# RMSNorm and GELU on one core: 48 KB row groups in four buffers, squares shared between ScalarE and VectorE, 1/rms mostly on VectorE, GELU in the group's own turn

## Chip, cores, metric

One core of a Trainium2 chip. The metric is device time in microseconds (us). A single-core program's runs are compared as they are: the granted clock was 1.00.

Short names: ACT is ScalarE, DVE is VectorE, POOL is GpSimd, SP is SyncE (it issues the loads).

## The reference

```python
# x: (8, 1024, 2048) float32, gamma: (2048,), eps = 1e-5
rms = np.sqrt(np.mean(x ** 2, axis=-1, keepdims=True) + eps)
out = gamma * x / rms
return 0.5 * out * (1 + np.tanh(np.sqrt(2 / np.pi) * (out + 0.044715 * out ** 3)))
```

8192 rows of 8 KB: 67.11 MB are read, 67.11 MB written.

## The kernel before

Each of the 128 partitions holds four rows of a group (32 KB); 16 groups go through six buffers. ACT squares and sums each row, POOL makes 1/rms from the four sums, DVE multiplies the rows by gamma in place, and ACT applies GELU with 1/rms as its scale, one group behind the squares.

```python
def scale(g):                      # DVE, in place, gamma broadcast in PSUM
    for r, n in scale_pieces.get(g, [(0, R)]):
        rows = slot[g % SLOTS][:, r : r + n, :]
        nc.vector.tensor_tensor(out=rows, in0=rows, in1=gamma_ps..., op=ALU.mult)
# ... squares (ACT, accum_out=ssq), inverse_rms (six small operations on POOL) cut
for g in range(G + 1):
    if g < G:
        squares(g)
        inverse_rms(g)
        scale(g)
    if g:
        gelu_store(g - 1)                  # one group behind
        if g - 1 + SLOTS < G:
            load(g - 1 + SLOTS)            # when the store has left the buffer
```

Of the kernel before, what the change touches and what calls it, by code (L numbers as in the profile page):

```python
# [1 line left out]

# [4 lines left out]

FP32 = mybir.dt.float32
ALU = mybir.AluOpType
ACT = mybir.ActivationFunctionType  # L10

P = 128
ROWS = 4
SLOTS = 6

GW = 32
CHUNK = 512

NARROW = 128


@with_exitstack
def kernel(
    ctx: ExitStack,
    tc: tile.TileContext,
    x: bass.AP,
    gamma: bass.AP,
    eps: bass.AP,
    out: bass.AP,
):  # L30




    nc = tc.nc
    D = x.shape[-1]
    R = ROWS
    eps_f = float(eps)
    x3 = x.rearrange("b s d -> (b s) d").rearrange("(g p r) d -> g p r d", p=P, r=R)
    o3 = out.rearrange("b s d -> (b s) d").rearrange("(g p r) d -> g p r d", p=P, r=R)  # L40
    G = x3.shape[0]

    sbuf = ctx.enter_context(tc.tile_pool(name="sbuf", bufs=1))
    psum = ctx.enter_context(
        tc.tile_pool(name="psum", bufs=1, space=bass.MemoryType.PSUM)
    )
    slot = [sbuf.tile([P, R, D], FP32, name=f"slot{i}") for i in range(SLOTS)]
    gamma_row = sbuf.tile([1, D // GW, GW + 4], FP32, name="gamma_row")
    ones = sbuf.tile([1, P], FP32, name="ones")
    warm = sbuf.tile([1, 1], FP32, name="warm")  # L50
    power = sbuf.tile([P, R], FP32, name="power")
    ssq = sbuf.tile([P, G, R], FP32, name="ssq")
    rstd = sbuf.tile([P, G, R], FP32, name="rstd")
    ms = sbuf.tile([P, R], FP32, name="ms")
    y = sbuf.tile([P, R], FP32, name="y")
    z = sbuf.tile([P, R], FP32, name="z")
    gamma_ps = psum.tile([P, D], FP32, name="gamma_ps")
    junk = psum.tile([P, D], FP32, name="junk")


    whole = [(R, [(0, R * D)])]
    store_pieces = {
        0: [(R, [(0, NARROW), (NARROW, R * D)])],
        G - 1: [(1, [(r * D, r * D + D)]) for r in range(R)],
    }
    scale_pieces = {G - 1: [(0, 1), (1, 1), (2, 1), (3, 1)]}

    def load(g):
        nc.sync.dma_start(out=slot[g % SLOTS], in_=x3[g])  # L69

    def squares(g):
        for r in range(R):
            nc.scalar.activation(  # L73
                out=junk,
                in_=slot[g % SLOTS][:, r, :],
                func=ACT.Square,
                accum_out=ssq[:, g, r : r + 1],
            )

    def scale(g):  # L80
        for r, n in scale_pieces.get(g, [(0, R)]):
            rows = slot[g % SLOTS][:, r : r + n, :]
            nc.vector.tensor_tensor(  # L83
                out=rows,
                in0=rows,
                in1=gamma_ps.unsqueeze(1).to_broadcast([P, n, D]),
                op=ALU.mult,
            )

    def inverse_rms(g):  # L90

        v = nc.gpsimd
        v.tensor_scalar(  # L93
            out=ms, in0=ssq[:, g, :], scalar1=1.0 / D, scalar2=eps_f,
            op0=ALU.mult, op1=ALU.add,
        )
        v.tensor_tensor(out=y, in0=ms, in1=power, op=ALU.pow)  # L97
        v.tensor_tensor(out=z, in0=y, in1=y, op=ALU.mult)  # L98
        v.tensor_tensor(out=z, in0=z, in1=ms, op=ALU.mult)  # L99
        v.tensor_scalar(  # L100
            out=z, in0=z, scalar1=-0.5, scalar2=1.5, op0=ALU.mult, op1=ALU.add
        )
        v.tensor_tensor(out=rstd[:, g, :], in0=z, in1=y, op=ALU.mult)  # L103

    def gelu_store(g):
        flat = slot[g % SLOTS].rearrange("p r d -> p (r d)")
        dst = o3[g].rearrange("p r d -> p (r d)")
        row = 0
        for n, stores in store_pieces.get(g, whole):
            for r in range(row, row + n):  # L110
                nc.scalar.activation(  # L111
                    out=slot[g % SLOTS][:, r, :],
                    in_=slot[g % SLOTS][:, r, :],
                    func=ACT.Gelu_apprx_tanh,
                    scale=rstd[:, g, r : r + 1],
                )
            row += n
            for a, b in stores:
                nc.scalar.dma_start(out=dst[:, a:b], in_=flat[:, a:b])  # L119

    with tc.manual_schedule():
        for k in range(0, D, CHUNK):
            nc.scalar.dma_start(
                out=gamma_row[:, k // GW : (k + CHUNK) // GW, 0:GW],
                in_=gamma[k : k + CHUNK].rearrange("(o a b) -> o a b", o=1, b=GW),
            )
        for g in range(SLOTS):
            load(g)
        nc.gpsimd.memset(power, -0.5)  # L129
        nc.vector.memset(warm, 0.0)  # L130
        nc.vector.memset(ones, 1.0)  # L131
        nc.scalar.activation(out=warm, in_=warm, func=ACT.Gelu_apprx_tanh)  # L132
        for k in range(0, D, CHUNK):
            nc.tensor.matmul(  # L134
                out=gamma_ps[:, k : k + CHUNK],
                lhsT=ones,
                rhs=gamma_row[:, k // GW : (k + CHUNK) // GW, 0:GW],
                start=True,
                stop=True,
            )  # L140
        for g in range(G + 1):
            if g < G:
                squares(g)
                inverse_rms(g)
                scale(g)
            if g:
                gelu_store(g - 1)
                if g - 1 + SLOTS < G:
                    load(g - 1 + SLOTS)


# [1 line left out]
_INS = ['x', 'gamma', 'eps']  # L153
_OUTS = [((8, 1024, 2048), 'float32')]

_NUMBERS = {'eps': 9.999999747378752e-06}


# [26 lines left out]
```

## Time and profile before

| before | value | how to read it |
|---|---|---|
| time | 317.45 us (317.38 to 317.48, 3 runs) | median |
| span of the profiled run | 315.5 us | what the profile covers |
| ACT / DVE / POOL busy | 251.2 / 139.4 / 32.3 us | shares 80, 44, 10% |
| DMA queues busy | 49.7 + 49.4% of 16 engines | loads and stores; nothing is left over |

The kernel is at the rate of the DMA from the second to the last but one of 40 slices. The prediction below shows the lines.

### The profile page before, as it was taken

To read this page: it belongs to the slowest core of one execution; us is meant where nothing else is said; L and a number is where in the kernel's file an instruction comes from. 1 tells how busy PE (TensorE), PEld (TensorE's weight loads), DVE (VectorE), ACT (ScalarE), POOL (GpSimd) and SP (SyncE) were. 2 spreads that over 40 slices of the span, in tenths; PEclk is the share of its full clock that TensorE was granted. 3 is DMA by queue.
4 is the path that set the end of the run, shared out by engine and by line. 5 is a ranking of instruction groups with operands and counts; after the bars stand their busy time and mean duration, and the time that the engine had idled before them with its cause. 6 is when DMAs were issued, how large, how long until landed. Compare 5 with 4: busy or idle time off the path is not lost.

```text
span 315.5 us, 479 instructions
## 1 busy us (share of the span) xinstructions
PE 7.9 (3%) x8; PEld 2.1 (1%) x8; DVE 139.4 (44%) x21; ACT 251.2 (80%) x194; POOL 32.3 (10%) x101
## 2 busy tenths in 40 slices
PE   0810000000000000000000000000000000000000
PEld 0200000000000000000000000000000000000000
DVE  0028909091918282827328082370824609480000
ACT  1289999999999999989596895969959599598500
POOL 0020202020202020202020020200202002020000
DMA  8999999999999999999999999999999999999997
GB/s 329 404 461 403 459 413 396 453 406 462 403 461 407 457 407 458 411 453 416 449 428 440 432 432 432 432 440 424 446 416 453 411 453 411 453 415 449 416 418 314
DMA packets 5315, 134.25 MB, mean 426 GB/s; under 512 B 704, under 2 KB 832, under 8 KB 832
## 3 DMA queue, kind: packets, MB, share of 16 engines
q1 hardware_dynamic: 2304, 67.11, 49.7%
q10 hardware_dynamic: 3008, 67.12, 49.4%
q14 instruction: 3, 0.02, 0.0%
HBM read 67.12 MB, written 67.11 MB: 425 GB/s over the span
## 4 chain that ended last, share of the span: by engine, by line
ACT 38%; DMA 32%; another core or an unknown queue 18%; issue 5%; ACTq 1%; SPq 0%
ACT slot L111 21%; DMA slot<-in_x_dram 16%; ACT junk L73 16%; DMA out_dram<-slot 15%; ACTq L119 1%; SPq L69 0%; ACTq L111 0%; ACTq L73 0%
## 5 line engine op out<-in xcount | busy, mean ns | idle before, releaser
L83 DVE TENSOR_TENSOR slot<-slot,gamma_ps 128x8192 f32<-128x8192 f32 (+1 forms) x19 | 139.2, 7338 | 142.3 <-ACT junk L73 142.3
L73 ACT ACTIVATE junk<-slot 128x2048 f32<-128x2048 f32 x64 | 120.4, 1881 | 40.8 <-DMA slot<-in_x_dram 36.8
L111 ACT ACTIVATE slot<-slot,rstd 128x2048 f32<-128x2048 f32 x64 | 123.0, 1987 | 1.7 <-ACT slot L111 1.7
L93 POOL TENSOR_SCALAR ms<-ssq 128x4 f32<-128x4 f32 x16 | 3.1, 194 | 242.8 <-ACT junk L73 242.8
L97 POOL TENSOR_TENSOR y<-ms,power 128x4 f32<-128x4 f32 x16 | 16.1, 1009 | 1.3
L73 ACT ACTIVATION_READ_ACCUMULATOR junk<-slot 128x1 f32 x64 | 11.9, 186 | 0.0
L134 PE MATMUL gamma_ps<-gamma_row,ones 1*128 1x512 f32 x8 | 7.9, 1112 | 9.2 <-DMA gamma_row<-in_gamma_dram 9.2
L132 ACT ACT_TABLE_LOAD x1 | 1.3, 1283 | 3.3 <-issue 3.3
L99 POOL TENSOR_TENSOR z<-z,ms 128x4 f32<-128x4 f32 x16 | 3.2, 201 | 1.3
L103 POOL TENSOR_TENSOR rstd<-z,y 128x4 f32<-128x4 f32 x16 | 3.2, 200 | 1.3
L98 POOL TENSOR_TENSOR z<-y 128x4 f32<-128x4 f32 x16 | 3.2, 200 | 1.3
L100 POOL TENSOR_SCALAR z<-z 128x4 f32<-128x4 f32 x16 | 3.1, 195 | 1.4
L134 PEld LDWEIGHTS gamma_ps<-gamma_row,ones 1*128 1x128 f32 x8 | 2.1, 306 | 13.4 <-issue 8.7
L130 DVE MEMSET warm<- 1x1 f32 x1 | 0.1, 59 | 0.8 <-PEq L166 0.8
L132 ACT ACTIVATE warm<-warm 1x1 f32<-1x1 f32 x1 | 0.2, 203 | 0.0
L131 DVE MEMSET ones<- 1x128 f32 x1 | 0.2, 165 | 0.0
L129 POOL MEMSET power<- 128x4 f32 x1 | 0.1, 102 | 0.3 <-POOLq L166 0.3
L166 POOL MEMSET const-float32-0.0<- 128x1 f32 x1 | 0.1, 99 | 0.2 <-issue 0.2
L166 POOL MEMSET const-bfloat16-1.0<- 128x1 bf16 x1 | 0.1, 102 | 0.0
L166 POOL MEMSET const-uint8-127<- 128x1 uint8 x1 | 0.1, 102 | 0.0
L166 POOL MEMSET const-float32-1.0<- 128x1 f32 x1 | 0.1, 99 | 0.0
## 6 DMA issues: line engine op xcount, KB each, us to landing
slot<-in_x_dram SPq DMA_DIRECT2D x16, 4096.0 KB, 29.9
out_dram<-slot ACTq DMA_DIRECT2D x14, 4096.0 KB, 43.3
out_dram<-slot ACTq DMA_DIRECT2D x4, 1024.0 KB, 17.5
out_dram<-slot ACTq DMA_DIRECT2D x1, 4032.0 KB, 28.5
gamma_row<-in_gamma_dram ACTq DMA_DIRECT2D x4, 2.0 KB, 10.3
out_dram<-slot ACTq DMA_DIRECT2D x1, 64.0 KB, 14.4
```

The lines of the kernel that those rows point to most:

```text
L73: nc.scalar.activation(out=junk, in_=slot[g % SLOTS][:, r, :], func=ACT.Square, accum_out=ssq[:, g, r : r + 1],)
L83: nc.vector.tensor_tensor(out=rows, in0=rows, in1=gamma_ps.unsqueeze(1).to_broadcast([P, n, D]), op=ALU.mult,)
L93: v.tensor_scalar(out=ms, in0=ssq[:, g, :], scalar1=1.0 / D, scalar2=eps_f, op0=ALU.mult, op1=ALU.add,)
L97: v.tensor_tensor(out=y, in0=ms, in1=power, op=ALU.pow)
L98: v.tensor_tensor(out=z, in0=y, in1=y, op=ALU.mult)
L99: v.tensor_tensor(out=z, in0=z, in1=ms, op=ALU.mult)
L100: v.tensor_scalar(out=z, in0=z, scalar1=-0.5, scalar2=1.5, op0=ALU.mult, op1=ALU.add)
L103: v.tensor_tensor(out=rstd[:, g, :], in0=z, in1=y, op=ALU.mult)
L111: nc.scalar.activation(out=slot[g % SLOTS][:, r, :], in_=slot[g % SLOTS][:, r, :], func=ACT.Gelu_apprx_tanh, scale=rstd[:, g, r : r + 1],)
L119: nc.scalar.dma_start(out=dst[:, a:b], in_=flat[:, a:b])
L132: nc.scalar.activation(out=warm, in_=warm, func=ACT.Gelu_apprx_tanh)
L134: nc.tensor.matmul(out=gamma_ps[:, k : k + CHUNK], lhsT=ones, rhs=gamma_row[:, k // GW : (k + CHUNK) // GW, 0:GW], start=True, stop=True,)
```

## The change

It brings fewer and larger packets, less work for ACT (17 of 64 squares per partition move to DVE), 1/rms on DVE with only the power left on POOL, one store for the last group. Buffers stay at 192 KB (4 x 48 instead of 6 x 32). With groups this large, GELU no longer runs one group behind.

```diff
-ROWS = 4
-SLOTS = 6
+ROWS = 6          # ten groups of six rows, a last one of four
+UNIT = 3
+SLOTS = 4
...
+    def squares_on_vector(g, r, n):        # one DVE scalar_tensor_tensor per row
...
     def inverse_rms(g):
-        v = nc.gpsimd                      # six operations, all on POOL
+        v = nc.vector                      # first and last three here,
+        nc.gpsimd.tensor_tensor(out=y_, in0=m_, in1=power..., op=ALU.pow)  # power on POOL
...
-        for g in range(G + 1):
-            if g < G:
-                squares(g); inverse_rms(g); scale(g)
-            if g:
-                gelu_store(g - 1)          # and the next load
+        for g in range(G):
+            n = rows[g]
+            mine = n - (1 if g % 2 else 2)
+            squares(g, 0, mine)                     # ACT: first rows
+            squares_on_vector(g, mine, n - mine)    # DVE: last one or two
+            half = UNIT if n == ROWS else 1
+            scale(g, 0, half)                       # DVE
+            inverse_rms(g)                          # DVE, POOL, DVE
+            for r in range(half, n, half):
+                scale(g, r, half)                   # DVE
+            gelu(g, 0, n)                           # ACT, same group
+            store(g, 0, n * D)                      # (group 0: in two pieces)
+            if g + SLOTS < G:
+                load(g + SLOTS, 0, rows[g + SLOTS])
```

(Cut with `...`; statements that only wrap lines are joined, and the comments are added here. The four small loads of gamma also became one.)

More of the change, by code (lines that the diff above doesn't have):

```diff
@@ L12 @@
 P = 128
-ROWS = 4
-SLOTS = 6
-GW = 32
-CHUNK = 512
+ROWS = 6
+UNIT = 3
+SLOTS = 4
+GW = 128
 NARROW = 128
@@ L36, with part @@
     D = x.shape[-1]
-    R = ROWS
     eps_f = float(eps)
-    x3 = x.rearrange("b s d -> (b s) d").rearrange("(g p r) d -> g p r d", p=P, r=R)
-    o3 = out.rearrange("b s d -> (b s) d").rearrange("(g p r) d -> g p r d", p=P, r=R)
-    G = x3.shape[0]
+    x2 = x.rearrange("b s d -> (b s) d")
+    o2 = out.rearrange("b s d -> (b s) d")
+    N = x2.shape[0] // P
+    rows = [ROWS] * (N // ROWS) + ([N % ROWS] if N % ROWS else [])
+    G = len(rows)
+    def part(a, g):
+        first = g * ROWS * P
+        return a[first : first + rows[g] * P].rearrange("(p r) d -> p r d", p=P)
     sbuf = ctx.enter_context(tc.tile_pool(name="sbuf", bufs=1))
@@ L46 @@
     )
-    slot = [sbuf.tile([P, R, D], FP32, name=f"slot{i}") for i in range(SLOTS)]
-    gamma_row = sbuf.tile([1, D // GW, GW + 4], FP32, name="gamma_row")
+    slot = [sbuf.tile([P, ROWS, D], FP32, name=f"slot{i}") for i in range(SLOTS)]
+    spare = sbuf.tile([P, D // GW, GW + 16], FP32, name="spare")
+    gamma_row = spare[0:1]
     ones = sbuf.tile([1, P], FP32, name="ones")
     warm = sbuf.tile([1, 1], FP32, name="warm")
-    power = sbuf.tile([P, R], FP32, name="power")
-    ssq = sbuf.tile([P, G, R], FP32, name="ssq")
@@ L53 @@
-    rstd = sbuf.tile([P, G, R], FP32, name="rstd")
-    ms = sbuf.tile([P, R], FP32, name="ms")
-    y = sbuf.tile([P, R], FP32, name="y")
-    z = sbuf.tile([P, R], FP32, name="z")
+    power = sbuf.tile([P, ROWS], FP32, name="power")
+    ssq = sbuf.tile([P, G, ROWS], FP32, name="ssq")
+    rstd = sbuf.tile([P, G, ROWS], FP32, name="rstd")
+    ms = sbuf.tile([P, ROWS], FP32, name="ms")
+    y = sbuf.tile([P, ROWS], FP32, name="y")
+    z = sbuf.tile([P, ROWS], FP32, name="z")
     gamma_ps = psum.tile([P, D], FP32, name="gamma_ps")
@@ L58, with load @@
     junk = psum.tile([P, D], FP32, name="junk")
-    whole = [(R, [(0, R * D)])]
-    store_pieces = {
-        0: [(R, [(0, NARROW), (NARROW, R * D)])],
-        G - 1: [(1, [(r * D, r * D + D)]) for r in range(R)],
-    }
-    scale_pieces = {G - 1: [(0, 1), (1, 1), (2, 1), (3, 1)]}
-    def load(g):
-        nc.sync.dma_start(out=slot[g % SLOTS], in_=x3[g])
-    def squares(g):
-        for r in range(R):
+    def load(g, r, n):
+        nc.sync.dma_start(
+            out=slot[g % SLOTS][:, r : r + n, :], in_=part(x2, g)[:, r : r + n, :]
+        )
@@ L73, in squares @@
+    def squares(g, r, n):
+        for q in range(r, r + n):
             nc.scalar.activation(
                 out=junk,
-                in_=slot[g % SLOTS][:, r, :],
+                in_=slot[g % SLOTS][:, q, :],
                 func=ACT.Square,
-                accum_out=ssq[:, g, r : r + 1],
+                accum_out=ssq[:, g, q : q + 1],
             )
-    def scale(g):
-        for r, n in scale_pieces.get(g, [(0, R)]):
-            rows = slot[g % SLOTS][:, r : r + n, :]
-            nc.vector.tensor_tensor(
-                out=rows,
-                in0=rows,
-                in1=gamma_ps.unsqueeze(1).to_broadcast([P, n, D]),
-                op=ALU.mult,
+    def squares_on_vector(g, r, n):
+        for q in range(r, r + n):
+            row = slot[g % SLOTS][:, q, :].rearrange("p (a b) -> p a b", b=GW)
+            nc.vector.scalar_tensor_tensor(
+                out=spare[:, :, 0:GW], in0=row, scalar=1.0, in1=row,
+                op0=ALU.bypass, op1=ALU.mult, accum_out=ssq[:, g, q : q + 1],
@@ L88, in scale @@
             )
     def inverse_rms(g):
-        v = nc.gpsimd
+        v = nc.vector
         v.tensor_scalar(
-            out=ms, in0=ssq[:, g, :], scalar1=1.0 / D, scalar2=eps_f,
-            op0=ALU.mult, op1=ALU.add,
-        )
-        v.tensor_tensor(out=y, in0=ms, in1=power, op=ALU.pow)
-        v.tensor_tensor(out=z, in0=y, in1=y, op=ALU.mult)
-        v.tensor_tensor(out=z, in0=z, in1=ms, op=ALU.mult)
-        v.tensor_scalar(
-            out=z, in0=z, scalar1=-0.5, scalar2=1.5, op0=ALU.mult, op1=ALU.add
-        )
@@ L103, in inverse_rms @@
-        v.tensor_tensor(out=rstd[:, g, :], in0=z, in1=y, op=ALU.mult)
-    def gelu_store(g):
-        flat = slot[g % SLOTS].rearrange("p r d -> p (r d)")
-        dst = o3[g].rearrange("p r d -> p (r d)")
-        row = 0
-        for n, stores in store_pieces.get(g, whole):
-            for r in range(row, row + n):
-                nc.scalar.activation(
-                    out=slot[g % SLOTS][:, r, :],
-                    in_=slot[g % SLOTS][:, r, :],
-                    func=ACT.Gelu_apprx_tanh,
-                    scale=rstd[:, g, r : r + 1],
-                )
-            row += n
-            for a, b in stores:
-                nc.scalar.dma_start(out=dst[:, a:b], in_=flat[:, a:b])
@@ L121 @@
-    with tc.manual_schedule():
-        for k in range(0, D, CHUNK):
-            nc.scalar.dma_start(
-                out=gamma_row[:, k // GW : (k + CHUNK) // GW, 0:GW],
-                in_=gamma[k : k + CHUNK].rearrange("(o a b) -> o a b", o=1, b=GW),
-            )
+            out=ms[:, 0 : rows[g]], in0=ssq[:, g, 0 : rows[g]], scalar1=1.0 / D,
+            scalar2=eps_f, op0=ALU.mult, op1=ALU.add,
+        )
+        m_, y_, z_ = ms[:, 0 : rows[g]], y[:, 0 : rows[g]], z[:, 0 : rows[g]]
@@ new lines, in inverse_rms, with scale @@
+        nc.gpsimd.tensor_tensor(
+            out=y_, in0=m_, in1=power[:, 0 : rows[g]], op=ALU.pow
+        )
+        v.tensor_tensor(out=z_, in0=m_, in1=y_, op=ALU.mult)
+        v.scalar_tensor_tensor(
+            out=z_, in0=z_, scalar=-0.5, in1=y_, op0=ALU.mult, op1=ALU.mult
+        )
+        v.scalar_tensor_tensor(
+            out=rstd[:, g, 0 : rows[g]], in0=z_, scalar=1.5, in1=y_,
+            op0=ALU.add, op1=ALU.mult,
+        )
+    def scale(g, r, n):
+        data = slot[g % SLOTS][:, r : r + n, :]
+        nc.vector.tensor_tensor(
+            out=data,
+            in0=data,
+            in1=gamma_ps.unsqueeze(1).to_broadcast([P, n, D]),
+            op=ALU.mult,
+        )
@@ new lines, in gelu, with store @@
+    def gelu(g, r, n):
+        for q in range(r, r + n):
+            row = slot[g % SLOTS][:, q, :]
+            nc.scalar.activation(
+                out=row, in_=row, func=ACT.Gelu_apprx_tanh,
+                scale=rstd[:, g, q : q + 1],
+            )
+    def store(g, a, b):
+        flat = slot[g % SLOTS].rearrange("p r d -> p (r d)")
+        dst = part(o2, g).rearrange("p r d -> p (r d)")
+        nc.scalar.dma_start(out=dst[:, a:b], in_=flat[:, a:b])
+    with tc.manual_schedule():
+        nc.scalar.dma_start(
+            out=gamma_row[:, :, 0:GW],
+            in_=gamma.rearrange("(o a b) -> o a b", o=1, b=GW),
+        )
@@ L127 @@
         for g in range(SLOTS):
-            load(g)
+            load(g, 0, rows[g])
         nc.gpsimd.memset(power, -0.5)
@@ L132 @@
         nc.scalar.activation(out=warm, in_=warm, func=ACT.Gelu_apprx_tanh)
-        for k in range(0, D, CHUNK):
+        for k in range(0, D, 512):
             nc.tensor.matmul(
-                out=gamma_ps[:, k : k + CHUNK],
+                out=gamma_ps[:, k : k + 512],
                 lhsT=ones,
-                rhs=gamma_row[:, k // GW : (k + CHUNK) // GW, 0:GW],
+                rhs=gamma_row[:, k // GW : (k + 512) // GW, 0:GW],
                 start=True,
@@ L140 @@
             )
-        for g in range(G + 1):
-            if g < G:
-                squares(g)
-                inverse_rms(g)
-                scale(g)
-            if g:
-                gelu_store(g - 1)
-                if g - 1 + SLOTS < G:
-                    load(g - 1 + SLOTS)
+        for g in range(G):
[9 more added lines that the diff above has]
+            gelu(g, 0, n)
+            if g == 0:
+                store(g, 0, NARROW)
+                store(g, NARROW, n * D)
+            else:
+                store(g, 0, n * D)
+            if g + SLOTS < G:
+                load(g + SLOTS, 0, rows[g + SLOTS])
 _INS = ['x', 'gamma', 'eps']
```

## The prediction

> **What bounds the kernel now.** I read the engine rows and the DMA row first. The busy line of the page, then its DMA rows and queue rows:
>
> ```profile
> PE 7.9 (3%) x8; PEld 2.1 (1%) x8; DVE 139.4 (44%) x21; ACT 251.2 (80%) x194; POOL 32.3 (10%) x101
> ...
> DMA  8999999999999999999999999999999999999997
> ...
> DMA packets 5315, 134.25 MB, mean 426 GB/s; under 512 B 704, under 2 KB 832, under 8 KB 832
> ...
> q1 hardware_dynamic: 2304, 67.11, 49.7%
> q10 hardware_dynamic: 3008, 67.12, 49.4%
> ```
>
> The busiest compute engine is ACT with 80%, but the 16 DMA engines are at nine tenths or more in 38 of 40 slices; only the first and the last are lower. The two queues (q1 loads, q10 stores) take 49.7 + 49.4 = 99.1% of what 16 engines have in the span of 315.5 us. Is the rate inside that full row steady, or are there slow stretches? The windows view, each line with its stretch in us, engine times, and at the end the DMA share and GB/s:
>
> ```profile
> 80.00:160.00 80.00, 0.00 (x0) 0.00 (x0) 42.90 (x5) 73.82 (x57) 9.60 (x29) 1.00 1.00 433
> 160.00:240.00 80.00, 0.00 (x0) 0.00 (x0) 34.75 (x4) 64.83 (x51) 7.99 (x24) 1.00 1.00 433
> 240.00:300.00 60.00, 0.00 (x0) 0.00 (x0) 26.25 (x6) 47.72 (x34) 5.99 (x18) 1.00 1.00 433
> ```
>
> 433 GB/s at a share of 1.00, whether loads and stores mix (80 to 240) or mostly stores run (after 280). 134.25 MB / 433 GB/s is 310.0 us; so 315.5 - 310.0 = 5.5 us are all that lies outside full rate. The trace has one record for each packet. Their durations sum to 312.9 us per engine, so an engine is without a packet for only 2.6 us, at the two ends: the first data packets start 1.7 us in and run 1.3 to 2.2 us where later ones take 1.213, and the last end about 1 us before the span does. Who waits for whom (engine line <- releaser: us, times, longest), first the compute engines', then the load issuer's:
>
> ```profile
> POOL ms L93 <- ACT junk L73: 242.8, 16, 20.8
> DVE slot L83 <- ACT junk L73: 142.3, 16, 20.6
> ACT junk L73 <- DMA slot<-in_x_dram: 36.8, 10, 8.7
> ...
> SPq L69 <- DMA out_dram<-slot: 224.3, 10, 53.7
> ```
>
> POOL and DVE wait for ACT, ACT waits for loads, and loads wait until a store has emptied the buffer. Each wait ends in the DMA. The 38% that the chain of waits gives ACT is the early part of that chain, at a time when 24 MB of loads are queued: it costs nothing.
>
> **What the Trainium skill says.** "DMA: Bandwidth & Descriptors", Specifications, puts the SBUF fabric ceiling at 435 GB/s; the 433 above agrees, so no room is left in the rate. The same page, "Queues, rings and completion order", says that each engine goes round robin between its queues packet by packet: two busy queues then share, and one alone gets everything. The trace agrees: the first four loads land 9.69 us apart (4.19 MB / 9.69 us = 433 GB/s), and with stores beside them 19.36 us apart, exactly half. The same page, "Why small descriptors are slow", has a fixed cost per packet on the engine's internal bus; the trace shows a fixed cost too: an 8 KB packet takes 309 ns (median), a 32 KB one 1213 ns, so (4 x 309 - 1213) / 3 = 7.7 ns per packet, and 1205 ns for 32 KB of data. "Vector Engine (DVE) Microarchitecture Reference", "Points that are easy to get wrong", warns that the scalar-tensor-tensor shape runs at half throughput with two sources in SBUF that are not bf16. The 17 new squares have this form; nothing in this trace measures it.
>
> **The change, part by part.**
>
> *Bytes:* unchanged, 67.11 MB each way. *Packets:* one per partition and row group. Data packets before: 16 loads x 128 of 32 KB; stores 14 x 128 of 32 KB, 128 of 31.5 KB, 128 of 512 B and 512 of 8 KB: 4608. After, with ten groups of six rows and one of four: loads 11 x 128, stores 12 x 128 (group 0 still has its narrow piece): 2944. Saved 1664 x 7.7 ns / 16 engines = 0.80 us. The small completion packets, 16 for each transfer at 9 ns each, go from 40 transfers to 24 (gamma from four to one): 16 x 9 ns = 0.14 us per engine. Together 0.94 us off the only busy resource. A 48 KB packet should take 1.5 x 1205 + 7.7 = 1816 ns.
>
> *ACT:* 17 of 64 squares leave: 17 x (1.881 + 0.186) = 35.1 us, so 251.2 - 35.1 = 216 us. This lies beside DMA time and shortens nothing by itself; ACT waits for loads longer instead. *DVE:* the scale costs 8687 ns for 8192 elements and 2278 for 2048, so 1.043 ns per element and 142 ns fixed: three rows 6.55 us, 20 of these plus 4 of 2.28 are 140 us, as before. The squares add 17 x 2.28 = 39 us at one element per cycle, or 17 x 4.4 = 75 us at half rate (I take this slower one as likely), and the small operations some 6 us: 185 to 221 us, under 70%. *POOL:* only the power, 11 x 1.01 us. The chain from the last square to 1/rms was 2.4 us (21.66 to 24.07 in group 0, six instructions with gaps of 0.1); now one DVE operation, the power and three DVE operations, about 2 us. Also hidden.
>
> *Buffers:* 6 x 32 KB becomes 4 x 48 KB: the same 192 KB. A shared group takes 2 x 6.29 MB / 433 GB/s = 29.1 us, so a buffer comes round every 4 x 29.1 = 116 us, as before (6 x 19.36 = 116). Of these the load and the store take at least 29.1 each. The compute between them, for a group of even number: two squares on DVE 8.8, half a scale 6.55, 1/rms 2.0, then gelu: 3 rows x 1.9, at most 1 us of waiting for the second half, 3 x 1.9, issue 0.35: together about 30 us. For odd ones five squares on ACT 10.2 + 2.0 + 12.8 = 25 us. So 116 - 58 - 30 = 28 us, nearly a whole group, of slack stands in the queues. In before the compute part held a buffer longer, since gelu ran one group late.
>
> *Start:* group 0's 6.29 MB need 4.85 us more than its 4.19 did, so ACT starts at 13.47 + 4.85 = 18.3 instead of 13.5. Its store is issued about 30 us later, at 48. The four first loads keep the engines busy until 1.7 + 4 x 14.5 = 60. So they never run dry.
>
> *End:* bytes queued at the end hide the compute. By my timetable the last load (4 MB) lands near 272, with the stores of groups 8 and 9 and part of 7 still to run (about 34 us). After it: two squares on DVE 8.8, row scales 2.28 each, 1/rms 2.0, four gelus: under 22 us, so the last store is issued near 294 and starts near 304 behind the one of group 9. Here one store instead of four waits for all four rows, which costs nothing while some 10 us of other stores stand ahead of it.
>
> Sum: 317.45 - 0.94 = 316.5 us. Of the 1.7 us of slow packets at the ends and where stores set in, I assume nothing is gained or lost.
>
> **The rivals.** *Both queues empty at once.* With fewer and larger buffers a load issued on a store's landing could leave an empty moment of about 2 us per group (issue 0.33 plus the first packet), eleven times 20 us: 335 us or so. For it: the loads wait 224 us for stores already. Against it: the slack of 28 us above, and in the kernel before a load lands 29.9 us after its issue though its own share takes 19.36, so transfers do queue. *DVE becomes the bound.* With half-rate squares it has 20 us in a 29.1 us group (2 x 6.55 + 1.5 x 4.4 + 0.5); it would need squares of some 10 us each to pass the DMA. Then each us over adds ten: 10 to 20 us slower. *The tail is laid bare.* If queued stores at the last landing are 10 us fewer than in my timetable, the coarser last group shows: 2 to 6 us slower. *Larger packets move faster than I say, or ends shift.* Even at the ceiling, 134.2 MB / 435 GB/s = 308.5, plus 2.6 us idle, 0.7 of slow first packets, and the 2.0 between span and time: 313.8 us, 1.1% faster. So over 2% faster would need bytes to vanish. Conversely 48 KB packets could share worse or end unevenly among the engines by up to one packet (1.8 us).
>
> **Range and chances.** The gain is bounded by packets, the loss by a bubble at an end: 316.5, with 315.4 to 318.0 to hold it 8 times in 10. Over 2% faster is below 311.1, past what the rate allows: 1%. Over 2% slower, above 323.8, needs over 7 us of empty engines, which only the rivals give: 3%. Within 2%: 96%.
>
> **What would show it.** In the changed profile the DMA row should again be 9 from the second to the last but one slice, the middle windows 433 GB/s, 48 KB packets 1816 ns, 2944 data packets, and the two queues' shares again sum to about 99%. ACT should be near 216 us with more waiting for loads, DVE at 185 to 221, squares at 2.3 or 4.4 us each. Ten full groups should land 29.1 us apart in the middle. The last store's issue should come before the one ahead of it has drained. I am wrong if the DMA row shows a slice of 8 or less inside, if packets of 48 KB take over 1830 ns, or if ACT or DVE runs without waits at the end while DMA idles.

## The result, and the profile after

323.15 us (322.93 to 323.25, 4 runs) against 317.47 us for the kernel before in the same rounds: ratio 1.0173, 95% interval 1.0156 to 1.0191. A ratio here and below is the mean time of one kernel's fast runs over that of the other's of the same rounds, so not quite the ratio of the medians quoted. The kernel became 5.7 us slower where 0.9 us faster was foreseen, and the time is outside the range of 315.4 to 318.0.

The engine row, the DMA rows and the queue rows of the page after:

```profile
PE 7.2 (2%) x8; PEld 2.5 (1%) x8; DVE 183.9 (57%) x104; ACT 219.3 (68%) x160; POOL 14.5 (5%) x16
...
DMA  8999999999999999999999999999999999994997
GB/s 307 471 398 471 410 432 452 384 400 469 410 453 429 430 447 410 459 410 447 429 436 441 416 453 404 453 429 435 441 410 435 447 418 418 433 422 202 392 408 311
...
q1 hardware_dynamic: 1584, 67.11, 49.0%
q10 hardware_dynamic: 1760, 67.12, 48.4%
```

The busy times are near what was worked out (ACT 219.3 against 216, DVE 183.9 against 185 at the lower end). But the DMA row has a 4 in slice 37, near the end, with 202 GB/s, which the prediction had named as a sign of being wrong; the queue shares sum to 97.4% instead of 99.1. The same place by windows (stretch in us; PE, PEld, DVE, ACT, POOL busy; clock, DMA share, GB/s):

```profile
240.00:270.00 30.00, 0.00 (x0) 0.00 (x0) 15.81 (x8) 21.98 (x17) 1.32 (x1) 1.00 1.00 433
270.00:280.00 10.00, 0.00 (x0) 0.00 (x0) 6.64 (x2) 6.31 (x8) 0.85 (x1) 1.00 1.07 459
280.00:290.00 10.00, 0.00 (x0) 0.00 (x0) 9.39 (x7) 8.22 (x5) 0.47 (x1) 1.00 0.82 354
290.00:300.00 10.00, 0.00 (x0) 0.00 (x0) 5.02 (x8) 7.41 (x7) 1.01 (x1) 1.00 0.74 319
```

The trace's packet records sharpen this (durations per engine, clipped to 2 us steps). Between 288 and 296 us the engines have no packet for 4.7 us, and between 308 and 310 for another 0.6; in the rest of the run the idle time is 0.4 us longer than before. That is 5.7 us, and the span grew by 321.1 - 315.5 = 5.7 us (rounded from 5.69). So the loss lies in two holes of the DMA, late in the run. But where does their cause lie? The waits (engine line <- releaser: us, times, longest), those of the compute engines first, then that of the issuer of the loads:

```profile
DVE slot L113 <- ACT junk L76: 87.2, 11, 10.2
ACT slot L123 <- DVE rstd L106: 59.3, 11, 6.7
...
ACT junk L76 <- DMA slot<-in_x_dram: 15.6, 1, 15.6
...
SPq L70 <- DMA out_dram<-slot: 244.6, 8, 55.7
```

Before, ACT waited ten times for a load (36.8 us). After, it waits once, for the first. From then on ACT waits 59.3 us for 1/rms (L106) instead: a wait that was not in the list before. ACT with its waits has become a chain without slack from 18.4 us to the last store. One group of it, group 9, in the timeline (start, duration, instruction, in brackets the idle time before it and its releaser):

```profile
266.27 1.88 ACT L76 ACTIVATE junk<-slot 128x2048 f32<-128x2048 f32 x1 [0.41 <-ACT slot L123]
...
272.37 6.55 DVE L113 TENSOR_TENSOR slot<-slot,gamma_ps 128x6144 f32<-128x6144 f32 x1 [10.19 <-ACT junk L76]
...
276.22 0.19 ACT L76 ACTIVATION_READ_ACCUMULATOR junk<-slot 128x1 f32 x1
278.84 0.17 DVE L94 TENSOR_SCALAR ms<-ssq 128x6 f32<-128x6 f32 x1
279.15 1.32 POOL L99 TENSOR_TENSOR y<-ms,power 128x6 f32<-128x6 f32 x1 [26.24 <-DVE ms L94]
...
280.90 0.17 DVE L106 SCALAR_TENSOR_TENSOR rstd<-z,y 128x6 f32<-128x6 f32 x1
280.99 6.55 DVE L113 TENSOR_TENSOR slot<-slot,gamma_ps 128x6144 f32<-128x6144 f32 x1
281.11 5.79 ACT L123 ACTIVATE slot<-slot,rstd 128x2048 f32<-128x2048 f32 x3 [4.70 <-DVE rstd L106]
287.57 5.79 ACT L123 ACTIVATE slot<-slot,rstd 128x2048 f32<-128x2048 f32 x3 [0.68 <-DVE slot L113]
293.38 0.34 ACTq L132 DMA_DIRECT2D out_dram<-slot  x1
293.77 1.88 ACT L76 ACTIVATE junk<-slot 128x2048 f32<-128x2048 f32 x1 [0.41 <-ACT slot L123]
```

Read it downwards. The half scale (272.37) writes rows 0 to 2 in place, so it can't start before ACT has squared row 2, the third square. It occupies DVE for 6.55 us. ACT's last square is done at 276.4, but 1/rms, next in DVE's queue, starts only when the half scale is over, at 278.84. ACT stands still from 276.4 to 281.1. The whole group takes 293.77 - 266.27 = 27.5 us of ACT. In even groups ACT has one square less and waits 2.0 us more, so those take 27.5 too. Ten such groups: 18.4 + 10 x 27.5 = 293.4; the trace has 293.8. Group 10 adds 14.8 to the last store's issue (308.6), and the last packet of its 4 MB ends 11.3 later (319.9).

While loads and stores share the DMA, full groups land 29.1 us apart, so ACT gains 1.6 us per group on the loads. But it starts far behind them: the first loads have no stores beside them, so group 3 has landed at 66.7 us, and ACT begins it at 101.1. At group 9 the lag is still 9.4 us (256.9 and 266.3), and the last load meets ACT in the middle of that group. So a period just under 29.1 us was not enough. To meet each load up to the last one (first landing 18.4, last 281.5, ten groups) it would have to be about 26.3 us, an estimate from these times. The kernel before had that margin: 16.1 us of ACT per group (39.15 to 55.24) against landings 19.4 us apart. It had worked off its lag at group 8:

```profile
136.08 1.88 ACT L73 ACTIVATE junk<-slot 128x2048 f32<-128x2048 f32 x1 [0.82 <-DMA slot<-in_x_dram]
```

In the changed kernel the end lays the lag bare. The last load's packets end at 281.1, and from then stores alone need only 14.5 us per group (6.29 MB at 433 GB/s, an estimate), while ACT still delivers one every 27.5 us. Most engines have no packet of group 8's store left after 289.4 (the last ends at 292.0), and the store of group 9 is issued at 293.4: there is the first hole.

### The profile page after: what moved, and what is told of

Its sections match the earlier page's. It is cut to its first block, busy times and chain, and to the rows that moved or that the text cites. A ratio compares the mean times of both kernels' runs of the same rounds, so it can differ in the third digit from the quotient of the medians.

```text
span 321.1 us, 423 instructions
## 1 busy us (share of the span) xinstructions
PE 7.2 (2%) x8; PEld 2.5 (1%) x8; DVE 183.9 (57%) x104; ACT 219.3 (68%) x160; POOL 14.5 (5%) x16
## 4 chain that ended last, share of the span: by engine, by line
ACT 36%; DVE 24%; issue 24%; DMA 5%; POOL 4%; ACTq 1%; DVEq 1%; POOLq 0%
DVE slot L113 22%; ACT junk L76 19%; ACT slot L123 17%; DMA slot<-in_x_dram 5%; POOL y L99 4%; ACTq L132 1%; DVEq L201 1%; DVE z L102 1%; DVE z L103 1%; DVE ms L94 1%; DVE rstd L106 1%; POOLq L201 0%; POOLq L99 0%; ACTq L123 0%
## 5 line engine op out<-in xcount | busy, mean ns | idle before, releaser
L113 DVE TENSOR_TENSOR slot<-slot,gamma_ps 128x6144 f32<-128x6144 f32 (+1 forms) x24 | 140.0, 5839 | 87.2 <-ACT junk L76 87.2
L123 ACT ACTIVATE slot<-slot,rstd 128x2048 f32<-128x2048 f32 x64 | 123.7, 1992 | 67.0 <-DVE rstd L106 59.3
L76 ACT ACTIVATE junk<-slot 128x2048 f32<-128x2048 f32 x47 | 88.4, 1881 | 20.8 <-DMA slot<-in_x_dram 15.6
L86 DVE SCALAR_TENSOR_TENSOR spare<-slot 128x2048 f32<-128x2048 f32 x17 | 38.9, 2288 | 17.7 <-DMA slot<-in_x_dram 17.5
L99 POOL TENSOR_TENSOR y<-ms,power 128x6 f32<-128x6 f32 (+1 forms) x11 | 14.2, 1294 | 284.3 <-DVE ms L94 284.3
L102 DVE TENSOR_TENSOR z<-ms,y 128x6 f32<-128x6 f32 (+1 forms) x11 | 1.8, 167 | 16.2 <-POOL y L99 16.2
L76 ACT ACTIVATION_READ_ACCUMULATOR junk<-slot 128x1 f32 x47 | 8.8, 186 | 0.0
L146 PE MATMUL gamma_ps<-spare,ones 1*128 1x512 f32 x8 | 7.2, 1069 | 9.5 <-DMA spare<-in_gamma_dram 9.5
L146 PEld LDWEIGHTS gamma_ps<-spare,ones 1*128 1x128 f32 x8 | 2.5, 322 | 12.6 <-issue 12.6
L103 DVE SCALAR_TENSOR_TENSOR z<-z,y 128x6 f32<-128x6 f32 (+1 forms) x11 | 1.8, 166 | 0.4
L106 DVE SCALAR_TENSOR_TENSOR rstd<-z,y 128x6 f32<-128x6 f32 (+1 forms) x11 | 1.8, 166 | 0.4
```

Of the source, the lines that this page charges most:

```text
L76: nc.scalar.activation(out=junk, in_=slot[g % SLOTS][:, q, :], func=ACT.Square, accum_out=ssq[:, g, q : q + 1],)
L86: nc.vector.scalar_tensor_tensor(out=spare[:, :, 0:GW], in0=row, scalar=1.0, in1=row, op0=ALU.bypass, op1=ALU.mult, accum_out=ssq[:, g, q ...
L99: nc.gpsimd.tensor_tensor(out=y_, in0=m_, in1=power[:, 0 : rows[g]], op=ALU.pow)
L102: v.tensor_tensor(out=z_, in0=m_, in1=y_, op=ALU.mult)
L103: v.scalar_tensor_tensor(out=z_, in0=z_, scalar=-0.5, in1=y_, op0=ALU.mult, op1=ALU.mult)
L106: v.scalar_tensor_tensor(out=rstd[:, g, 0 : rows[g]], in0=z_, scalar=1.5, in1=y_, op0=ALU.add, op1=ALU.mult,)
```

## The experiments

**Theory:** the chain ACT - DVE - POOL - DVE - ACT inside each group is the bound: 27.5 us per group, ten groups, without overlap between groups. The holes at the end are only where it shows. **Rivals:** (A) the last group's form (4 rows, one store) makes the holes; (B) 48 KB groups in four buffers starve the queues; (C, D) it is ACT's total work, or the squares' work on DVE; later (E) only what follows the last load counts, (F) ACT's wait for 1/rms is the whole cause and its order on DVE the remedy, (G) no wait for row 2.

All kernels here gave correct results. Each is the changed kernel with one edit; each table entry is a median with the range of its fast runs, and the ratio is against the kernel before in the same rounds.

| run | edit | us | range | ratio to before (95%) |
|---|---|---|---|---|
| e1 | 1/rms all on POOL | 317.14 | 317.06 to 317.57 | 0.9987 (0.9965 to 1.0009) |
| e2 | squares all on ACT (full groups) | 322.06 | 321.93 to 322.10 | 1.0138 (1.0117 to 1.0159) |
| e3 | four stores for the last group | 322.64 | 322.37 to 322.81 | 1.0157 (1.0131 to 1.0183) |
| e4 | scales of two rows | 317.57 | 317.21 to 317.74 | 0.9996 (0.9974 to 1.0018) |
| e5 | 0.8 us more on DVE per group | 331.84 | 331.79 to 331.99 | 1.0455 (1.0439 to 1.0471) |
| e6 | 1/rms ahead of the scales | 355.47 | 355.38 to 355.59 | 1.1199 (1.1182 to 1.1216) |
| e7 | 4-row groups, six buffers | 331.95 | 331.80 to 331.99 | 1.0457 (1.0439 to 1.0474) |
| e8 | GELU one group behind | 321.13 | 320.71 to 323.00 | 1.0132 (1.0097 to 1.0167) |
| e9 | DVE squares the first rows | 317.79 | 317.13 to 318.85 | 1.0021 (1.0005 to 1.0036) |
| e10 | e1 and e9 together | 317.72 | 317.65 to 318.15 | 1.0016 (1.0004 to 1.0028) |

### e1: 1/rms back on GpSimd

```diff
-        v = nc.vector          # four operations on DVE, the power on POOL
+        v = nc.gpsimd          # the six operations of before, all on POOL
```

> Undoes one part: all of 1/rms is back on GpSimd, nothing else. Theory (the chain ACT-DVE inside one group is the bound, because 1/rms waits in VectorE's queue behind the 6.55 us half scale, which itself must wait for ACT's square of row 2): ACT's wait before the first gelu falls from 6.7/4.7 us to about 4.6/2.5, so a group takes 25.5 us of ACT instead of 27.5 and comes under the 29.1 us of its DMA; ACT begins to wait for loads again, DMA is full to the end, time 316.5 to 317.5 us. Rival A (the tail with its single store and 4-row group costs the 5.7 us): stays at 322 to 323.5. Rival B (48 KB groups in four buffers starve the queues): stays at 322 to 323.5.

317.14 us: the whole loss is gone by undoing one part of four. The waits in this run:

```profile
DVE slot L110 <- ACT junk L76: 59.8, 10, 10.1
DVE spare L86 <- DMA slot<-in_x_dram: 54.6, 7, 17.4
ACT junk L76 <- DMA slot<-in_x_dram: 25.8, 4, 15.4
ACT slot L120 <- POOL rstd L106: 16.7, 6, 2.8
```

ACT and DVE wait for loads again, four and seven times; the first line fell by 27 us. POOL takes longer for the chain (2.7 us from the last square, against DVE's and POOL's 2.3 once they begin), yet wins, since it doesn't stand behind a scale. Rivals A and B fall as sole causes: the tail and the buffers are those of after. (The edit also takes DVE's own wait for the power, some 1.5 us per group, out of its queue; e4 leaves both there.)

### e2: the squares back on ACT

```diff
-            mine = n - (1 if g % 2 else 2)
+            mine = n if n == ROWS else n - 2
```

> Undoes another part: in the ten 6-row groups all squares are back on ACT (the last group keeps its two on VectorE). ACT gets 31 us more work. Theory: no change, 323.2 +- 0.7 us, since the half scale starts after row 2's square and ends at 6.1 + 6.55 = 12.7 us after the group's first square in either case, and six squares take 12.2: the first gelu starts at the same moment; ACT's idle time before gelu falls by the 31 us that it works more. Rival C (ACT's total work is what counts): 340 to 354 us. Rival D (the squares on VectorE slow the chain): faster by 3 us or more.

322.06 us, 0.4 below the range given and 1.1 below after. ACT's busy time rose from 219.3 to 249.3 us, and its wait fell by the same 30:

```profile
ACT slot L123 <- DVE rstd L106: 28.8, 11, 2.7
```

The last store is issued at 308.4 us, after: 308.6. So the chain is the same, and the 1.1 us lie behind it: the last store landed 10.7 us after its issue instead of 11.3, the rest is the difference between rounds; I have no cause for it. Rival C falls: 30 us of ACT work cost nothing. Rival D, 3 us or more faster, falls at that size too. The other side of it: moving 17 squares to DVE could gain nothing in this order.

### e3: four stores for the last group

```diff
+            if g == G - 1:
+                for q in range(n):
+                    gelu(g, q, 1)
+                    store(g, q * D, q * D + D)
+                continue
```

> Undoes a third part: the last group's rows are stored one by one. Theory: only the second gap of the DMA (about 1.5 us near 309) closes: 321.3 to 322.3 us. Rival A (the tail's single store is the cause): 317 to 318.5.

322.64 us: 0.5 faster than after, 0.3 above the range. I had taken the second hole for 1.5 us; the packet records give 0.6, and it closed. The first hole stayed. Rival A is about a tenth of the loss.

### e4: scales of two rows

```diff
-UNIT = 3
+UNIT = 2
```

> A smaller first scale: three scales of two rows in place of two of three, all else as after the change. Theory: first scale starts after row 1's square and takes 4.4 us, so 1/rms comes 4.1 us (even) or 2.3 us (odd groups) earlier, each group costs ACT about 25 us, under the DMA's 29.1; time 316.5 to 317.5 us. Rivals A and B: stays at 322 to 323.5.

317.57 us, 0.1 above the range. ACT waited 29.3 us for 1/rms instead of 59.3 and five times for loads, as foreseen:

```profile
ACT junk L76 <- DMA slot<-in_x_dram: 32.5, 5, 15.4
ACT slot L123 <- DVE rstd L106: 29.3, 11, 3.4
```

This leaves 1/rms on DVE and shortens only what stands ahead of it: the place in the queue is the cost, not the engine.

### e5: the suspected cost made longer

```diff
             scale(g, 0, half)
+            if n == ROWS:
+                nc.vector.memset(spare[:, 0:7, 0:GW], 0.0)
             inverse_rms(g)
```

> A suspected cost made longer: one useless VectorE memset of 896 elements (about 0.9 us, its duration will be read) stands between the first half scale and 1/rms in each of the ten 6-row groups. Theory (the chain through ACT and VectorE is the bound from the first group to the last, since ACT never waits for a load after the first): all ten count, +8 to +10 us, 331 to 333.5 us. Rival E (only what follows the last load counts, the earlier groups are hidden beside DMA): at most two count, 323.5 to 325.5 us.

331.84 us. The added instruction, from the page of this run:

```profile
L161 DVE MEMSET spare<- 128x896 f32 x10 | 8.1, 805 | 1.4
```

ACT's wait for 1/rms rose by 68.2 - 59.3 = 8.9 us, and the time by 8.7: all ten groups count, so groups that ran 200 us before the holes delay the end as much as the last ones. Rival E (323.5 to 325.5) falls.

### e6: 1/rms ahead of both scales

```diff
-            scale(g, 0, half)
             inverse_rms(g)
+            scale(g, 0, half)
```

> Order alone: 1/rms ahead of both half scales on VectorE. Theory: 1/rms then comes 2.2 us after the last square, but the first half scale only begins after it, and the first gelu needs that too: first gelu 17 (even) or 19 us (odd) after the group's first square instead of 14.8, second half 6.5 us later, so a group takes 29.7 or 31.7 us instead of 27.5: +32 us, 350 to 357 us. A reader who takes 'ACT waits for 1/rms' as the whole cause (rival F) expects it faster than 323.

355.47 us. The tempting remedy costs 32 us. ACT's largest wait is now the one for the scale:

```profile
ACT slot L123 <- DVE slot L113: 99.4, 23, 8.8
```

The first GELU needs both 1/rms and the scaled rows. DVE does them one after the other, in either order; in the order of after, one scale at least overlaps ACT's squares. Rival F falls.

### e7: the group size put back (and one square of every group on VectorE)

```diff
-ROWS = 6
-UNIT = 3
-SLOTS = 4
+ROWS = 4
+UNIT = 2
+SLOTS = 6
-            mine = n - (1 if g % 2 else 2)
+            mine = n - 1
```

> The group size alone goes back: 4-row groups in six buffers (scales of two rows, one square of four on VectorE, all else as after). Theory: each group has its handoff, now for 4 rows: first half scale ends 8.4 us after the first square, 1/rms 1.9, two gelus, second half, two gelus: 19.0 us a group, 16 groups from 13.4: the last store at about 318: 327 to 333 us, slower still. Rival B (48 KB groups in four buffers are to blame): 316.5 to 318 us.

331.95 us: with smaller groups the same order is 9 us slower still, because each group has its handoff. Its last store was issued at 318.0 us, as worked out. Rival B, as the cause by itself, falls: large groups made the new order less bad.

### e8: GELU one group behind, with the large groups

```diff
-            gelu(g, 0, n)
-            ...                # store, next load
+            if g:
+                finish(g - 1)  # GELU, store and next load of the group before
+        finish(G - 1)
```

> The order of before put back: gelu and store run one group behind the squares, with all the rest of the change (48 KB, four buffers, squares and 1/rms on VectorE). Theory: ACT squares the next group while VectorE scales, so it no longer waits before gelu; a group costs ACT 21 us; a buffer is held for 29 + 51 + 29 = 109 us of the 116 that four groups take, so loads still suffice: 316.5 to 318 us. Rival B (four buffers are too few, now that each is held longer): 320 us or more.

321.13 us (three fast runs, 320.71 to 323.00; a fourth of 328.64 counts as slow and is left out, though the spread of the fast ones is already wider than any other kernel's here): my expectation failed and rival B's number came. ACT's wait for 1/rms is gone from the list; in its place stand loads:

```profile
ACT junk L76 <- DMA slot<-in_x_dram: 80.3, 9, 15.8
DVE spare L86 <- DMA slot<-in_x_dram: 71.2, 8, 17.6
```

Now the store of a group can't be issued before the next group has landed and been squared. The packet records show both queues empty for 2.1 us between 274 and 278 us: the store of group 7 landed at 275.8, the last load at 277.0, and the store of group 8 was issued at 277.0. A second hole of 1.2 us follows near 293. My 109 of 116 us treated a slack of 7 us on average as enough; it isn't when both queues end together. So in this run four buffers of 48 KB did not carry the order of before, and the change's own order does not hide the handoff. The two parts are linked: the new order goes with the larger groups. That the four buffers alone are to blame is read from this trace and was not tested by another run; a version that issues the store ahead of the next squares was not built.

### e9: VectorE squares the first rows

```diff
-            squares(g, 0, mine)
-            squares_on_vector(g, mine, n - mine)
+            squares_on_vector(g, 0, n - mine)
+            squares(g, n - mine, mine)
```

> One thing against after: VectorE squares the first one or two rows of a group instead of the last, ACT the rest; same counts, same bytes. Theory: the half scale of rows 0 to 2 overwrites x in place, so it waits for ACT's square of row 2. That is now ACT's first square (even groups) or second (odd), so the half scale ends 8.6 or 10.6 us after ACT's first square instead of 12.6, 1/rms follows, first gelu at 10.8 or 12.9 instead of 14.8: a group costs ACT 23.5 or 25.5 us instead of 27.5, under the DMA's 29.1: 316.5 to 317.6 us. If the half scale does not wait for that row (rival G: it is VectorE's own work ahead of 1/rms that counts), nothing moves: 322 to 323.5 us.

317.79 us, 0.2 above the range and 5.4 below after. The half scale starts 4.7 us after the group's first square in an even group near the end (231.54 after 226.82), where it now waits only for DVE's own squares, and 4.07 us in an odd one (259.80 after 255.73), after ACT's second square; in after it was 6.1 in both. I expected 2.0 for the even ones and had overlooked that DVE's two squares come first when both engines start at a load's landing.

```profile
231.54 6.55 DVE L113 TENSOR_TENSOR slot<-slot,gamma_ps 128x6144 f32<-128x6144 f32 x1
...
259.80 6.55 DVE L113 TENSOR_TENSOR slot<-slot,gamma_ps 128x6144 f32<-128x6144 f32 x1 [1.77 <-ACT junk L76]
```

Rival G falls: the same work with other rows makes the difference.

### e10: both repairs, to see whether anything beats the kernel before

> Both repairs: first rows squared on VectorE, 1/rms on GpSimd. Theory: each repair alone already brings the chain under the DMA, so the second gains nothing more: 316.5 to 317.4 us, and against before between 0 and 0.9 us faster, the packets' 0.94 us being all that is left of the change to gain.

317.72 us, 0.3 above the range, against 317.21 for before in the same rounds: 0.16% slower where 0 to 0.9 us faster was expected; the interval just excludes equality. Once the DMA is full again, the rest of the change shows no gain. No version here beats the kernel before clearly; e1 (0.9987) and e4 (0.9996) cannot be told from it. That the repairs work by the period shows in where ACT first waits for a load again: group 7 in e1 (197.3 us), group 6 in e4 (168.5) and e9 (168.6), never in after.

## Why the prediction was wrong, point by point

- **What bounds the kernel before: right.** The repaired kernels e1, e4, e9 and e10 have 31 to 33 us less work on ACT than before and 39 to 46 us more on DVE, and all end at 317.1 to 317.8.
- **Packets: right in size, but given back.** A 48 KB packet took 1815 ns (1816 foreseen); the number of data packets was 2944. By the usual duration of each size, the data packets sum to 310.78 us per engine before and 309.90 after, 0.88 less. But packets slower than usual took 1.47 us per engine before, 2.41 after, and 1.8 to 2.0 in e1, e4, e9 and e10. In those four, 0.9 to 1.2 us of it lie in loads at 50 to 60 us, where the first large store sets in (before: 0.7 at 45 to 56); after itself loses 0.85 there, and about 0.7 in scattered places later. I had assumed that nothing would be lost or gained. The full sum is 312.73 us against 312.91. Why larger load packets lose more there stays open.
- **ACT: the sum was near, its meaning was not.** "So 251.2 - 35.1 = 216 us. This lies beside DMA time and shortens nothing by itself; ACT waits for loads longer instead." The 219.3 measured lie, but for the first 1.5, in a chain of 290 us (18.4 to 308.6), 59.3 of it waits for 1/rms. Busy time told nothing about the room left. The prediction also read ACT's 38% of the chain of waits as an early part that "costs nothing"; that early part is where ACT works off its lag behind the first loads (to 136.1 us in before), and after this change it never did.
- **The step that failed: "Buffers".** It added the compute of a group as "two squares on DVE 8.8, half a scale 6.55, 1/rms 2.0, then gelu ..., together about 30 us" and set these against the 116 us in which a buffer comes round, as a delay with 28 us of slack. Two errors. First, with GELU in its own group, ACT does not begin the next group before this one is done, so the figure is not only a delay but a period; 30 us against the DMA's 29.1 should have been the alarm. It was 27.5, and even that was too long for ACT to work off its lag of 34 us at group 3, so the last store was issued at 308.6. Second, the terms were wrong: for even groups it let the half scale start right behind DVE's squares, though that scale is in place and has to wait for ACT's square of row 2; for odd groups it left out that 1/rms stands behind the half scale. The measured term: first gelu 14.8 us after the first square, in both. e9 tests the wait for row 2, e1 and e4 the queue behind the half scale, e5 that it is a period.
- **Squares at half rate: wrong,** 2.29 us, not 4.4. By the prediction's terms the first gelu comes 8.8 + 6.55 + 2.0 = 17.4 us after the first square in even groups and 10.2 + 2.0 = 12.2 in odd ones. Their mean is 14.8, and that of its 30 and 25 us per group is 27.5, both as measured: luck, for three wrong terms cancel.
- **End: wrong by this.** "The last load lands near 272" and "the last store is issued near 294": 281.1 and 308.6. At the last landing there were not 34 us of stores ahead of ACT but 8: ACT had been 9 to 34 us behind the loads in every group from the second on.
- **The rivals:** "The tail is laid bare", with "2 to 6 us slower", named the place and the size. It was set aside by the timetable of the failed step, so the range took in little of it. Its reason was not the coarser last group, which e3 shows to be worth 0.5 us, but the lag of ACT.

## What to carry to other kernels

Busy shares say how much work an engine has, not whether it has room: when one group's steps hop between engines and the next group starts only afterwards, add up the chain of one group with its waits, and compare that period with what the bound engine needs for a group. It must lie below that by enough to work off what the chain is behind at the start, or the rest shows in the tail, where stores alone took about half the time of a shared group here (14.5 against 29.1 us, as worked out above). Small operations that release another engine should not stand behind a long one in the queue of theirs, and an in-place operation waits for the readers of what it overwrites: which rows go to which engine decided 5.4 us here. Letting one step run a group behind (software pipelining) holds buffers longer; in e8 four of them were, as far as its trace shows, too few.

## What the Trainium skill lacked or had wrong

- "Vector Engine (DVE) Microarchitecture Reference", "Points that are easy to get wrong": half throughput for a scalar-tensor-tensor with two sources in SBUF that are not bf16. Not so here: with float32, the same row as both inputs and an accumulated sum, 2048 elements took 2.29 us, as much as the multiply with gamma from PSUM (2.28), plus 0.08 for reading the accumulator.
- "VectorE: DVE Perf Modes", "Zero memsets can be issued as uint32 (trn2)": one cycle per element, which at the page's 0.96 GHz is 933 ns for 896 elements. The memset of e5 took 805 ns in all. With the 165 ns of a memset of 128 elements in the same run, that is 0.83 ns per element.
- "GPSIMD Engine Reference" has no cost for the power: 1.01 us for 4 columns and 1.32 for 6, so 0.16 us per column, while POOL's other small operations took 0.20 us for either.
- No page tells of the slow stretch where stores set in beside queued loads: 0.7 to 0.8 us per engine with 32 KB packets (before, e7), 0.9 to 1.2 with 48 KB ones, with single packets up to 1.9 times their usual time (e2).
